# Spatial weights of the samples turned by VectorE, and a new place for the first four samples' attention values

## The chip, the core and the metric

The kernel runs on one core of a Trainium2 chip. The metric is the device time of one execution in microseconds (us), as the median over several executions; smaller is better. Before the change the three executions took 1272.37, 1272.98 and 1273.51 us, a median of 1272.98 us.

## The reference, cut to what matters

One step of a two-layer encoder for two groups of requests that share the weights: one prompt of 512 tokens, and 8 samples of 16 new tokens each. Both layers are 1024 wide with a branch of 2048.

Layer 0 mixes tokens by spatial weights. There are 16 groups of 128 channels, each with its own 128 x 128 matrix. The prompt uses the masked matrix over blocks of 128 tokens; a sample has only 16 tokens, so it uses the upper left 16 x 16 corner:

```python
wm = where(chunk_causal_mask(n)[None], w_s[:, :n, :n], 0.0)
s = einsum('gij,bnjgc->bnigc', wm, vb) + b_s[:, :n].T
y = u * s.reshape(B, T, E) * silu(z)
```

Layer 1 is attention with a forgetting bias, 16 heads of 128. The prompt attends causally to itself. Every sample attends to 256 cached rows of K and V and to its own 16 new ones:

```python
s = einsum('bqhd,bkhd->bhqk', q, k) * scale
s = s + cT[:, :, P:, None] - cT[:, :, None, :]
p = softmax(where(mask, s, -inf))
out = einsum('bhqk,bkhd->bqhd', p, v)
```

## The kernel before, in words

The tokens are five tiles of 128: four of the prompt, and one that holds the 8 samples with 16 rows each. All large matmuls take float32 operands that are split into a high and a low part, and issue three matmuls per product (`mm3`, L272, L273, L274). `split` makes the parts: ScalarE (ACT) copies the high part (L289), VectorE (DVE) subtracts it to get the low part (L290). The projections go by `seven_products`, a scheme with seven instead of eight products of quarter matrices; its sums stand on DVE (L713, L724, L726, L729) and some sums of weights on GpSimd (POOL, L211). Weights come by DMAs that POOL's queue or SyncE's (SP's) queue issues.

**Layer 0.** For each of the 16 groups g `spatial_weights(g)` makes the two right operands of `gate_spatial(g)`. The 128 x 128 matrix is loaded as it lies in memory, transposed by the TensorE (PE, L688) and copied out of PSUM (`wm`, L690, L691). For the samples, eight DMAs put the 16 x 16 corners of all groups into the tile `w16`, once for each sample's 16 partitions. `spatial_weights` multiplies one group of `w16`, repeated along the row, by a block mask on DVE (L684), which gives a block-diagonal 128 x 128 matrix `ax`. The PE transposes it (L689) and ACT copies it into `ws` (L692), the operand of the sample tile's matmul.

**Layer 1.** The heads go in eight pairs p. For p from 0 to 6 a loop interleaves the projections of this pair's gates and the next pair's V, K and Q, which are long rows of `mm3`, with short *pieces*, each of which has a due time in us from the pair's start. Pieces of the prompt: scores, softmax, turn (the PE transposes the weights, L1186) and values (L1193), block by block for each head; for the weights DVE takes a reciprocal (L1179) and scales (L1180), 128 to 512 columns wide with the block. Pieces of the samples, made by `sample_pieces(p, bg)` for two groups of four samples, bg = 0 and 1: *scores* (eight matmuls that each use 32 columns of the array, L1243, and a softmax on DVE and ACT), *turn* (three transposes, L1262), *values* (twelve matmuls of 32 columns, L1270, which are ordered one behind another) and *gate* (two transposes, L1278, and DVE L1284). The samples' K is loaded by `load_k`, transposed by DVE in 32 x 32 blocks (`turn_k`, L1219) and completed with new rows by POOL (`new_k`); V comes by `load_v`, two DMAs for four samples. `turn_v` is the PE's transposing of the next pair's projected V (L1071, L1076). The last pair's pieces are placed between the matmuls of the kernel's tail.

**Order.** A scheduler with a model of its own decides in which order the instructions of each engine go out; the due times steer it. `queued(e)` puts an instruction behind the last one issued on engine e; `tc.issue_after` says that a later instruction may not go ahead of an earlier one. Neither says that nothing else may come between. The PSUM banks of the pieces come from a ring of three (`ATT`).

## Time and profile before

| | before |
|---|---|
| median of three executions | 1272.98 us (1272.37 to 1273.51) |
| the profiled execution | 1273.51 us |
| its span from first to last instruction | 1271.6 us |
| granted PE clock | 1.00 |
| PE busy | 1264.2 us (99%) |
| DVE busy | 957.1 us (75%) |
| ACT busy | 594.6 us (47%) |
| POOL busy | 356.2 us (28%) |

The page gives for each engine the busy time, its share of the span and the number of instructions; the PE line is the sum of time in which matmuls run, and rows in a timeline are start and duration in us, engine, line, operation, the tile written and the tile read, and behind them the idle time of the engine just before with what ended it. Matmuls overlap, so the spacing of their starts tells more than their durations. Layer 0's groups with spatial weights run from about 120 to 345 us of the span, the seven pairs of heads of the loop from about 585 to 1060 us.

### The profile page before, as it was taken

To read this page: it belongs to the slowest core of one execution; us is meant where nothing else is said; L and a number is where in the kernel's file an instruction comes from. 1 tells how busy PE (TensorE), PEld (TensorE's weight loads), DVE (VectorE), ACT (ScalarE), POOL (GpSimd) and SP (SyncE) were. 2 spreads that over 40 slices of the span, in tenths; PEclk is the share of its full clock that TensorE was granted. 3 is DMA by queue.
4 is the path that set the end of the run, shared out by engine and by line. 5 is a ranking of instruction groups with operands and counts; after the bars stand their busy time and mean duration, and the time that the engine had idled before them with its cause. 6 is when DMAs were issued, how large, how long until landed. Compare 5 with 4: busy or idle time off the path is not lost.

```text
span 1271.6 us, 21433 instructions
## 1 busy us (share of the span) xinstructions
PE 1264.2 (99%) x8038; PEld 1136.5 (89%) x8038; DVE 957.1 (75%) x1795; ACT 594.6 (47%) x1076; POOL 356.2 (28%) x323
## 2 busy tenths in 40 slices
PE   9999999999999999999999999999999999999998
PEld 7888999999988888889999999999999998788887
DVE  6844999999953364789988998989898988545643
ACT  4433555544545343665445454545454445454331
POOL 1012445454000010145434535454435430000100
PEclk9999999999999999999999999999999999999999
DMA  5532343323324212657798858677888659632211
GB/s 201 174 98 78 108 127 112 103 80 104 114 94 144 94 44 84 150 127 157 173 167 168 195 150 186 157 172 142 151 168 179 177 110 283 230 129 84 67 66 50
DMA packets 275545, 171.54 MB, mean 135 GB/s; under 512 B 188721, under 2 KB 238689, under 8 KB 275442
## 3 DMA queue, kind: packets, MB, share of 16 engines
q1 hardware_dynamic: 261170, 127.80, 36.9%
q0 software_dynamic: 9760, 36.05, 13.7%
q10 hardware_dynamic: 4512, 6.33, 1.7%
q8 instruction: 63, 1.03, 0.3%
q14 instruction: 40, 0.33, 0.1%
HBM read 148.55 MB, written 21.59 MB: 134 GB/s over the span
## 4 chain that ended last, share of the span: by engine, by line
PE 97%; DVE 2%; issue 0%; ACT 0%; ACTq 0%; DVEq 0%
PE pb L272 27%; PE pb L274 27%; PE pb L273 27%; PE pb L1193 3%; PE pb L1270 2%; PE pb L419 2%; PE pb L1186 1%; PE pb L1243 1%; PE pb L317 1%; PE pb L745 1%; PE pb L1058 1%; DVE W L290 1%; PE pb L1071 1%; PE pb L1262 0%; PE pb L1059 0%
## 5 line engine op out<-in xcount | busy, mean ns | idle before, releaser
L272 PE MATMUL pb<-A,W 128*128 128x320 f32 (+1 forms) x752 | 240.7, 320 | 0.0
L273 PE MATMUL pb<-A,W 128*128 128x320 f32 (+1 forms) x752 | 233.7, 311 | 0.0
L274 PE MATMUL pb<-A,W 128*128 128x320 f32 (+1 forms) x752 | 233.2, 310 | 0.0
L290 DVE TENSOR_TENSOR W<-RAW,W 128x1024 fp32r<-128x1024 f32 (+1 forms) x122 | 149.6, 1227 | 71.9 <-ACT W L289 69.7
L273 PE MATMUL pb<-W,A 128*128 128x512 f32 x498 | 194.5, 391 | 0.0
L272 PE MATMUL pb<-W,A 128*128 128x512 f32 x498 | 194.5, 393 | 0.0
L274 PE MATMUL pb<-W,A 128*128 128x512 f32 x498 | 194.3, 391 | 0.0
L289 ACT ACTIVATE W<-RAW 128x1024 fp32r<-128x1024 f32 (+1 forms) x122 | 115.8, 949 | 90.0 <-PE pb L274 43.9
L272 PEld LDWEIGHTS pb<-A,W 128*128 128x128 f32 x752 | 141.6, 188 | 1.0 <-issue 0.2
L273 PEld LDWEIGHTS pb<-A,W 128*128 128x128 f32 x752 | 141.6, 188 | 0.5
L274 PEld LDWEIGHTS pb<-A,W 128*128 128x128 f32 x752 | 141.2, 188 | 0.0
L272 PE MATMUL pb<-tbf,W 128*128 128x320 f32 x360 | 118.9, 330 | 0.4 <-DVE R L1099 0.4
L303 POOL TENSOR_TENSOR SML<-SML 128x1 f32<-128x1 f32 x20 | 14.9, 749 | 350.9 <-DVE SML L301 346.2
L274 PE MATMUL pb<-tbf,W 128*128 128x320 f32 x360 | 111.3, 309 | 0.0
L273 PE MATMUL pb<-tbf,W 128*128 128x320 f32 x360 | 111.2, 309 | 0.0
L274 PEld LDWEIGHTS pb<-W,A 128*128 128x128 f32 x498 | 93.4, 188 | 19.6 <-issue 0.4
L273 PEld LDWEIGHTS pb<-W,A 128*128 128x128 f32 x498 | 93.6, 188 | 18.7
L272 PEld LDWEIGHTS pb<-W,A 128*128 128x128 f32 x498 | 93.5, 188 | 18.5
L211 POOL TENSOR_TENSOR sff<-RAW 128x512 f32<-128x512 f32 x46 | 61.2, 1330 | 169.3 <-DVE W L290 90.7
L713 DVE TENSOR_TENSOR R<-R,pb 128x320 f32<-128x320 f32 x184 | 86.3, 477 | 12.8 <-PE pb L274 11.7
L290 DVE TENSOR_TENSOR A<-R,A 128x640 fp32r<-128x640 f32 (+1 forms) x42 | 35.5, 880 | 57.8 <-ACT A L289 57.8
L272 PEld LDWEIGHTS pb<-tbf,W 128*128 128x128 f32 x360 | 67.7, 188 | 10.3 <-issue 5.8
(270 smaller groups left out, 2842.2 us busy)
## 6 DMA issues: line engine op xcount, KB each, us to landing
RAW<-in_fox_w_in POOLq DMA_DIRECT2D x46, 512.0 KB, 7.5
RAW<-in_gmlp_w_in SPq DMA_DIRECT2D x40, 512.0 KB
R<-in_cache_fox_k SPq DMA_DIRECT2D x128, 128.0 KB
R<-in_cache_fox_v SPq DMA_DIRECT2D x32, 512.0 KB
RAW<-in_gmlp_w_out SPq DMA_DIRECT2D x16, 512.0 KB
RAW<-in_ple_w_gate SPq DMA_DIRECT2D x16, 512.0 KB
RAW<-in_fox_w_out SPq DMA_DIRECT2D x16, 512.0 KB
R<-in_fox_w_in POOLq DMA_DIRECT2D x14, 512.0 KB, 8.5
```

What stands on the lines that cost most here:

```text
L211: nc.gpsimd.tensor_tensor(out=o, in0=a, in1=b, op=op)
L272: nc.tensor.matmul(out, lh, rh, start=start, stop=False)
L273: nc.tensor.matmul(out, lh, rl, start=False, stop=False)
L274: nc.tensor.matmul(out, ll, rh, start=False, stop=stop)
L289: first = nc.scalar.activation(out=hi, in_=src, func=AF.Copy)
L290: nc.vector.tensor_tensor(out=lo, in0=src, in1=f(hi), op=ALU.subtract)
L303: behind["pool"] = nc.gpsimd.tensor_tensor(out=q, in0=t, in1=mhalf, op=ALU.pow)
L317: behind["pe"] = nc.tensor.transpose(out=b[:, j * P:(j + 1) * P], in_=src[:, (4 * c + j) * P:(4 * c + j + 1) * P], identity=ident)
L419: line[e] = make(*args, **kw)
L713: behind["dve"] = nc.vector.tensor_tensor(out=into(i, j), in0=a, in1=b, op=ALU.add)
L1193: nc.tensor.matmul(O[:, d], v[:, j, hh * P:(hh + 1) * P], pt[:, j * P:(j + 1) * P], start=(j == 0), stop=(j == i))
L1270: last = nc.tensor.matmul(O[32 * bl:32 * bl + 32, :256], pt[:, t * P + 32 * bl:t * P + 32 * bl + 32], v_of(p)[:, 4] if t == 2 else vv[:, b ...
```

## The change

Two things are changed.

**In layer 0**, the corners are loaded so that a 32 x 32 block holds each one twice side by side (16 DMAs in place of 8), DVE transposes the whole 128 x 512 tile by 32 x 32 blocks in one instruction, and ACT copies every block's left half into `w16`. `w16` then holds turned corners, and the product with the block mask goes straight into `ws`. The 16 transposes L689 and the 16 copies L692 are gone.

**In layer 1**, for p from 0 to 6, the values of group 0 are moved from their due time 17.5 to 26.0 us, and the score matmuls of group 1 are made part of the same ordered chain: `values(products)` issues the twelve value matmuls and then, in the same `issue_after` stack, the eight score matmuls. The gate of group 0 moves from 22.5 to 28.5, the softmax of group 1 to 28.6, the load of group 1's V from 18.5 to 26.1 (it overwrites the tile that the values of group 0 read), and the two `turn_v` from 26.0 and 27.0 to 28.7 and 29.7. The softmax's reciprocal gets its own two columns in the tile `SML`. The score matmuls of every call are now in an ordered chain.

```diff
-    SML = sbuf.tile([P, N_SMALL], F32, name="SML")
+    SML = sbuf.tile([P, N_SMALL + 2], F32, name="SML")
...
+    twice, turned_twice = r1(o_u, 512), r1(o_u + 512, 512)
     for b in range(NB):
-        dma(w16[b * TS:(b + 1) * TS], w_s[0, :, :TS, :TS].rearrange("g i j -> i g j"))
+        for z in range(2):
+            dma(twice.rearrange("p (g z j) -> z p g j", g=16, z=2)[z, b * TS:(b + 1) * TS], w_s[0, :, :TS, :TS].rearrange("g i j -> i g j"))
+    with queued("dve"):
+        nc.vector.transpose(out=turned_twice, in_=twice)
+    nc.scalar.activation(out=w16, in_=turned_twice.rearrange("p (g z i) -> p g z i", g=16, z=2)[:, :, 0], func=AF.Copy)
...
         nc.vector.tensor_tensor(
-            out=ax.rearrange("p (b j) -> p b j", b=NB), in0=blk.rearrange("p (b j) -> p b j", b=NB),
+            out=ws.rearrange("p (b j) -> p b j", b=NB), in0=blk.rearrange("p (b j) -> p b j", b=NB),
             in1=w16[:, g:g + 1, :].broadcast_to([P, NB, TS]), op=ALU.mult)
         b = bank(SPA)
         nc.tensor.transpose(out=b[:, :P], in_=raw, identity=ident)
-        nc.tensor.transpose(out=b[:, P:2 * P], in_=ax, identity=ident)
...
-        nc.scalar.activation(out=ws, in_=b[:, P:2 * P], func=AF.Copy)
...
-        def scores():
-            S = bank(ATT)
+        def products(stack):
+            S = kept["S"] = bank(ATT)
+            for hh in range(2):
+                for bl in range(4):
+                    last = nc.tensor.matmul(S[32 * bl:32 * bl + 32, :272], qpads[:, hh, 4 * bg + bl].rearrange("p h q -> p (h q)"),
+                                            kt[:, hh, bl], start=(hh == 0), stop=(hh == 1))
+                    stack.enter_context(tc.issue_after(last.ins))
+
+        def weigh():
+            S = kept["S"]
...
-            m, sm, ri = small(), small(), small()
+            m, sm, ri = small(), small(), SML[:, N_SMALL + bg:N_SMALL + bg + 1]
...
-        def values():
+        def scores():
+            with ExitStack() as stack:
+                products(stack)
+            weigh()
+
+        def values(follow=None):
...
+                if follow is not None:
+                    follow(stack)
...
-    def sample_times(p, bg, t0):
-        scores, turn, values, gate = sample_pieces(p, bg)
-        return [(t0, scores), (t0 + 7.5, turn), (t0 + 12.5, values), (t0 + 17.5, gate)]
+    def sample_times(p, s0, s1):
+        scores, turn, values, gate, _, _ = sample_pieces(p, 0)
+        scores1, turn1, values1, gate1, products, weigh = sample_pieces(p, 1)
...
+        return [(s0, scores), (s0 + 7.5, turn), (s1, lambda: values(products)), (s1 + 2.5, gate), (s1 + 2.6, weigh),
+                (s1 + 7.5, turn1), (s1 + 12.5, values1), (s1 + 17.5, gate1)]
...
-                   (s0 + kb + 0.1, lambda: new_k(p, 1)), (s0 + 13.5, lambda: load_v(p, 1))]
+                   (s0 + kb + 0.1, lambda: new_k(p, 1)), ((s0 + 13.5 if p == 7 else s1 + 0.1), lambda: load_v(p, 1))]
...
-        pieces += [(26.0, lambda p=p: turn_v(p + 1, 0)), (27.0, lambda p=p: turn_v(p + 1, 1))]
+        pieces += [(28.7, lambda p=p: turn_v(p + 1, 0)), (29.7, lambda p=p: turn_v(p + 1, 1))]
```

The scheduler's rows show where the pieces come to stand. (Line numbers of the changed kernel are a few higher: L1270 becomes L1282, L1243 becomes L1244, L1186 becomes L1189, L1193 becomes L1196, L1180 becomes L1183.)

On the PE, in every pair of the loop, the values of group 0 (L1270) stood like this between projection matmuls, with two of the prompt's transposes among them:

```order
L274 MATMUL pb1_71<-A_65,W_63 128x320
L1270 MATMUL pb4_74<-R1_69 32x256 x4
L1186 MATMUL pb6_76<-CST_67,R1_69 128x128 x2
L1270 MATMUL pb4_74<-R1_69 32x256 x8
L272 MATMUL pb2_72<-tbf_4177,W_63 128x320
```

Now the values of group 0 (L1282) and, behind them, the scores of group 1 (L1244), the prompt's transposes L1189 and values L1196 stand like this:

```order
L274 MATMUL pb2_72<-A_65,W_63 128x320
L1282 MATMUL pb5_75<-R1_69 32x256 x12
L272 MATMUL pb2_72<-A_65,W_63 128x320
L1189 MATMUL pb4_74<-CST_67,R1_69 128x128 x4
L273 MATMUL pb2_72<-A_65,W_63 128x320
L274 MATMUL pb2_72<-A_65,W_63 128x320
L1196 MATMUL pb7_77<-R1_69 128x128
L1244 MATMUL pb6_76<-R1_69 32x272 x8
L1196 MATMUL pb7_77<-R1_69 128x128 x2
L272 MATMUL pb3_73<-tbf_4155,W_63 128x320
```

The twelve value matmuls are together, and five other rows stand between them and the eight score matmuls, which are inside the prompt's values.

On DVE, the stretch before the prompt's fourth block of weights (L1180, 128x512) in pair 1 was:

```order
L1179 RECIPROCAL SML_68<-SML_68 128x1
L713 TENSOR_TENSOR R1_69<-R1_69,pb3_73 128x320
L1219 STREAM_TRANSPOSE R1_69<-R1_69 128x256 x4
L1180 TENSOR_SCALAR R1_69<-R1_69,SML_68 128x512
L290 TENSOR_TENSOR W_63<-sff_4178,W_63 128x1024
L713 TENSOR_TENSOR R1_69<-R1_69,pb0_70 128x320
L1159 TENSOR_TENSOR R1_69<-CST_67 128x128
```

and is now:

```order
L716 TENSOR_TENSOR R1_69<-R1_69,pb3_73 128x320
L1222 STREAM_TRANSPOSE R1_69<-R1_69 128x256 x4
L290 TENSOR_TENSOR W_63<-sff_4156,W_63 128x1024
L1182 RECIPROCAL SML_68<-SML_68 128x1
L716 TENSOR_TENSOR R1_69<-R1_69,pb0_70 128x320
L1162 TENSOR_TENSOR R1_69<-CST_67 128x128
L1183 TENSOR_SCALAR R1_69<-R1_69,SML_68 128x512
```

The scaling of the fourth block went behind a subtraction of weights, a sum and a small operation.

On SP's queue, the loads of a pair were four of K, two of V, four of K, two of V, four of K; now they are:

```order
L124 DMA R1_69<-in_cache_fox_k 32x32x32 x4
L124 DMA R1_69<-in_cache_fox_v 128x4x256 x2
L124 DMA R1_69<-in_cache_fox_k 32x32x32 x8
L124 DMA R1_69<-in_cache_fox_v 128x4x256 x2
L124 DMA out_4<-R1_69 128x256 x4
```

The second V went behind the third load of K.

More of the change, by code (lines that the diff above doesn't have):

```diff
@@ L1285, in gate @@
                                                op0=ALU.mult, op1=ALU.mult)
-        return scores, turn, values, gate
+        return scores, turn, values, gate, products, weigh
     def prompt_times(h, t0, step):
```

11 lines of the change are left out of this document (5 added, 6 removed).

## Prediction

> **What bounds the kernel now.** I read the page first: span, busy shares and the chain of work that ended last.
>
> ```profile
> span 1271.6 us, 21433 instructions
> PE 1264.2 (99%) x8038; PEld 1136.5 (89%) x8038; DVE 957.1 (75%) x1795; ACT 594.6 (47%) x1076; POOL 356.2 (28%) x323
> PE 97%; DVE 2%; issue 0%; ACT 0%; ACTq 0%; DVEq 0%
> ```
>
> The PE is busy for 1264.2 of 1271.6 us and carries 97% of the chain. So a row taken off the PE shortens the kernel unless another engine steps in, and a row elsewhere costs only if it makes the PE wait. The two stages that the change touches come from the view by windows (window and length, then busy us and rows of PE, weight loads, DVE, ACT, POOL, then granted clock, DMA share and GB/s):
>
> ```profile
> 120.00:345.00 225.00, 224.53 (x1561) 222.63 (x1560) 210.44 (x329) 118.93 (x217) 93.52 (x61) 1.00 0.35 107
> 585.06:1059.74 474.68, 474.49 (x3628) 444.41 (x3627) 417.82 (x966) 228.56 (x454) 211.38 (x205) 1.00 0.78 165
> ```
>
> The first holds the sixteen groups of layer 0, the second the seven pairs of heads. In both the PE is full and at full clock, but DVE is close behind: 210.44/225.00 = 94% and 417.82/474.68 = 88%. Every term below is therefore PE time, and every danger is a DVE row that comes late.
>
> **Term a: sixteen transposes fewer.** One of them in the PE's timeline, between projection matmuls, and the group of all sixteen:
>
> ```profile
> 140.20 0.31 PE L274 MATMUL pb<-tb,W 128*128 128x320 f32 x1
> 140.49 0.31 PE L273 MATMUL pb<-A,W 128*128 128x320 f32 x1
> 140.64 0.31 PE L274 MATMUL pb<-A,W 128*128 128x320 f32 x1
> 140.79 0.27 PE L689 MATMUL pb<-CST,R 128*128 128x128 f32 x1
> 141.04 0.31 PE L273 MATMUL pb<-A,W 128*128 128x320 f32 x1
> L689 PE MATMUL pb<-CST,R x16: 270/270/272, 140.8 to 336.4; 128*128 128x128 f32 x16
> ```
>
> The row says 0.27 us, but matmuls overlap and the spacing of starts is what counts. From an L274 to the second row after it takes 140.49 − 140.20 = 0.29 us without a transpose, and 141.04 − 140.64 = 0.40 with L689 between. One costs 0.11; rounding leaves 0.10 to 0.11, and 16 × 0.105 gives **−1.7 us**. Whether the PE can use this depends on DVE:
>
> ```profile
> 142.42 0.49 DVE L726 TENSOR_TENSOR R<-R,pb 128x320 f32<-128x320 f32 x1 [0.58 <-PE pb L274]
> ```
>
> DVE waits 0.58 us for the PE's L274 just after this transpose. So it is the PE that is late there, and I book the whole term; its bounds are −1.7 and 0 (a rival below).
>
> **What term a adds** is hidden. The new DVE transpose reads 128x512; the nearest row is the larger block transpose of the 128x640:
>
> ```profile
> L1085 DVE STREAM_TRANSPOSE R<-R 128x640 f32<-128x640 f32 x16 | 13.3, 831 | 0.0
> ```
>
> So it costs under 0.83 us, once, near 126 us; the 0.58 us of DVE idle time above, and others like it, stand behind it. If that cover were gone it would cost the PE 0.83 us at most. ACT gains one copy and loses sixteen. The eight further DMAs are issued by SP's queue:
>
> ```profile
> 69.45 0.33 SPq L124 DMA_DIRECT2D R<-in_gmlp_b_s  x1
> 75.53 3.98 SPq L124 DMA_DIRECT2D RAW<-in_gmlp_w_in  x2
> ```
>
> At 0.33 us each, as the first row, they take 2.6 us, and between 69.45 + 0.33 = 69.78 and 75.53 the queue does nothing. Their data are wanted some 50 us later. I take 0.
>
> **Term b: the values of group 0 in one piece.** Before, two of the prompt's transposes split the twelve value matmuls of group 0 (the same order in all seven pairs); those of group 1 stand together. Pair 0 of the loop, both groups:
>
> ```profile
> 599.96 0.31 PE L274 MATMUL pb<-A,W 128*128 128x320 f32 x1
> 600.20 0.64 PE L1270 MATMUL pb<-R 128*32 128x256 f32 x8
> 600.77 0.44 PE L1186 MATMUL pb<-CST,R 128*128 128x128 f32 x2
> 601.13 1.07 PE L1270 MATMUL pb<-R 128*32 128x256 f32 x16
> 602.39 0.31 PE L273 MATMUL pb<-tbf,W 128*128 128x320 f32 x1
> ...
> 631.86 0.31 PE L274 MATMUL pb<-A,W 128*128 128x320 f32 x1
> 633.79 0.31 PE L273 MATMUL pb<-tbf,W 128*128 128x320 f32 x1
> ```
>
> Both times I measure from the L274 ahead to the L273 behind. Split: 602.39 − 599.96 = 2.43 us. Together: 633.79 − 631.86 = 1.93. Of the difference, 0.50, the two transposes are 2 × 0.105 = 0.21, which stay in the program; 0.29 is the price of entering and leaving 32-column work once more. Seven pairs: 7 × 0.29 = **−2.0 us**. The bounds are 0, if the new place splits them in another way, and −2.0; the printed order shows the twelve in one piece, so I take all of it.
>
> The Trainium skill (TensorEngine Tiling (Array Packing), Key Properties) says that a change of the tiling mode drains the TensorE. The 0.29 us agrees; the page has no price. By its rule the change's second half would pay too if the scores really followed the values, which is the rival "tied" below.
>
> **Term c: the scores leave into other work.** The order puts the eight scores of group 1 inside the prompt's values (L1196, two passes per matmul) instead of ahead of the transposes L1071. So the exit changes its neighbour. What that costs is not shown in the same place; nearest are values of the prompt alone and two-pass matmuls right behind scores:
>
> ```profile
> 613.38 0.83 PE L1193 MATMUL pb<-R 128*128 128x128 f32 x6
> 614.13 1.12 PE L1243 MATMUL pb<-R 128*32 128x272 f32 x16
> ...
> 1093.90 0.49 PE L1163 MATMUL pb<-R 128*128 128x128 f32 x2
> 1094.23 0.83 PE L1193 MATMUL pb<-R 128*128 128x128 f32 x6
> ```
>
> A row of the first kind takes (614.13 − 613.38)/6 = 0.125 us, so two take 0.25; behind scores two take 1094.23 − 1093.90 = 0.33. The exit costs 0.08 at most more than into transposes, and nothing if those pay it too: 0 to 7 × 0.08 = 0.6. With no reason for either end I take the middle, **+0.3 us**.
>
> **Term d: the prompt's fourth weights come later on DVE.** The order moves L1180 (128x512) behind L290, L713 and L1159. Pair 1 before on DVE, the four transposes L1186 that wait for it on the PE, and the same two in pair 2:
>
> ```profile
> 677.89 0.44 DVE L1180 TENSOR_SCALAR R<-R,SML 128x512 f32<-128x512 f32 x1
> 678.25 1.21 DVE L290 TENSOR_TENSOR W<-sff,W 128x1024 fp32r<-128x1024 f32 x1
> 679.39 0.47 DVE L713 TENSOR_TENSOR R<-R,pb 128x320 f32<-128x320 f32 x1
> 679.79 0.28 DVE L1159 TENSOR_TENSOR R<-CST 128x128 f32<-128x128 f32 x1
> 679.99 0.34 DVE L1284 SCALAR_TENSOR_TENSOR R<-pb,R 128x64 f32<-128x64 f32 x2
> ...
> 680.25 0.60 PE L1186 MATMUL pb<-CST,R 128*128 128x128 f32 x4
> ...
> 745.14 0.44 DVE L1180 TENSOR_SCALAR R<-R,SML 128x512 f32<-128x512 f32 x1
> ...
> 748.00 0.60 PE L1186 MATMUL pb<-CST,R 128*128 128x128 f32 x4
> ```
>
> The three rows now ahead take 679.99 − 678.25 = 1.74 us from start to start. The weights would start at 677.89 + 1.74 = 679.63 and end, after 0.44, at 680.07. The PE reached the transposes at 680.25; with the 0.29 of term b and two transposes (0.21) gone from ahead of it and one row (0.15, the spacing of 140.49 and 140.64) added, it arrives at 679.90: 0.17 us too early. In pair 2 the weights end at 745.14 + 1.74 + 0.44 = 747.32 and the PE comes at 748.00 − 0.35 = 747.65, which is 0.33 in time. Queued behind the moved row on DVE are sums of the projections and the smaller scores' rows; behind the waiting transposes on the PE is all of the projection. One pair late by 0.17 and one in time make 0.08 on average, times 7: **+0.5 us**, between 0 and 2.4 (all seven late by 0.17 and as much again for the hand-over, 0.34).
>
> **The moved V load.** It overwrites the tile that the values of group 0 read, so it goes out after them, and on SP's queue behind the third K load:
>
> ```profile
> 677.99 9.01 SPq L124 DMA_DIRECT2D R<-in_cache_fox_k  x4
> ...
> 699.85 1.50 PE L1270 MATMUL pb<-R 128*32 128x256 f32 x24
> ...
> R<-in_fox_w_in POOLq DMA_DIRECT2D x14, 512.0 KB, 8.5
> ```
>
> The K load's last issue ends at 677.99 + 9.01 = 687.00; V's two transfers, of 512 KB each, are wanted at 699.85. That leaves 12.8 us. The last row, from the list of DMA issues, is another transfer of that size: a median of 8.5 us from issue to landing. Side by side two of them fit; one after the other they take 17 and the PE would stand for 4.2 (a rival below). With the DMA engines busy for 0.78 of this stage there is room, and I take 0. The gate, the softmax and `turn_v` only move to later times with the same rows; `turn_v` is wanted by the next pair, tens of us later, and the softmax of group 1 by its turn at 33.5, some 5 us behind its scores. I take 0 for them.
>
> **Sum.** −1.7 − 2.0 + 0.3 + 0.5 = −2.9 us. The profiled execution took 1273.51 us (span 1271.6 and 1.9 around it), so its like would be at 1270.6. It was the slowest of the three, 0.5 above the median of 1272.98; from the median I predict **1270.1 us**. What a measurement here can tell from no change is about 0.2%, 2.5 us: below 1270.43 counts as faster, above 1275.53 as slower.
>
> **Rivals.**
>
> *DVE is late in every pair.* The fourth weights come late by 0.34 in all seven pairs, 2.4 us for the 0.5 of term d: 1270.1 + 1.9 = 1272.0. For it: DVE is 88% busy there and pair 1 is short already. Against it: pair 2 has 0.33 to spare.
>
> *Layer 0 is bound by DVE.* Then the PE waits where a transpose was and term a is 0: 1271.8. For it: 94% busy. Against it: DVE idles on the PE in the row at 142.42.
>
> *The stretch is really tied.* If nothing stood between the values and the scores on the chip's path, seven more entries and exits would go, again 7 × 0.29 = 2.0 us: 1268.1. Against it: the printed order has five rows in between, and engines execute in that order.
>
> *POOL stops DVE ahead of the fourth weights: slower.* This one is a single place, the L290 that the order has put ahead of the weights. A like row of the same line took three times as long when POOL was at work:
>
> ```profile
> 672.64 1.86 DVE L290 TENSOR_TENSOR W<-R,W 128x512 fp32r<-128x512 f32 x1
> 675.49 0.68 DVE L290 TENSOR_TENSOR W<-R,W 128x512 fp32r<-128x512 f32 x1
> ...
> 672.63 1.31 POOL L211 TENSOR_TENSOR sff<-RAW 128x512 f32<-128x512 f32 x1
> ```
>
> The price is 1.86 − 0.68 = 1.2 us. If the shifted times brought a POOL row beside that L290 in every pair, the weights would be 1.2 later and the PE would wait for all of it: 7 × 1.2 = 8.4 on top, 1278.5. It turns the gain to a loss from 2.9/7 = 0.41 us per pair, and past 0.2% from 5.4/7 = 0.77. Against it: the L290 at 678.25 took its 1.21 undisturbed, 4 us after POOL's row ended. The Trainium skill (SBUF — State Buffer, SBUF: two separate sides) says why: a DVE instruction with two SBUF inputs and a GpSimd instruction that reads SBUF take a shared port in turns, and the later one waits. The pair of rows agrees.
>
> *The V load is late: slower.* If the two transfers went one after the other, the PE would stand for 4.2 us in each pair, 29 us: 1299. Against it: the free fifth of the DMA engines' time, and that the two are issued together.
>
> **How the numbers follow.** The forecast 0.60; DVE late in every pair 0.13; layer 0 bound by DVE 0.10; POOL 0.08; tied 0.05; V late 0.04. The likeliest one's own range is 1269.3 to 1271.1 (term c from 0 to 0.6, term d from 0 to 1.2); about three quarters of it lie below 1270.43. Faster: 0.75 × 0.60 + 0.05 = 0.50. Slower: 0.08 + 0.04 = 0.12. The rest, 0.15 + 0.13 + 0.10 = 0.38, is no change to be told. The range from 1268.0 to 1274.0 holds the forecast, the tied case and both cases near 1272, 0.88 in all; its upper end stands for POOL in a pair or two.
>
> **What would show it.** Term a: no second transposes in the first window, and 1.7 us less from its first to its last group; if DVE binds, a longer idle of the PE that ends with a DVE row. Term b: the spacing from the row ahead of the twelve values to the second row behind them, 1.93 in place of 2.43. Term c: two L1196 rows behind the scores, 0.33 against 0.25. Term d: the idle time ahead of the four transposes L1189 in each pair, ended by DVE L1183: 0 to 0.2 us. V: no idle time of the PE ahead of group 1's values that a DMA ends. The prediction is wrong if the period of the pairs, from one group-0 turn to the next, does not shrink by 0.2 us or so, or if a new idle of the PE of over 0.4 us stands in each pair.

## The result and the profile after

The change made the kernel slower: 1294.17 us median (1290.88 to 1295.28) against 1273.24 us for the kernel before on the same chip (1272.37 to 1274.01). The ratio is 1.016 with a 95% interval of 1.0146 to 1.0174, or 20.9 us more; 1270.1 was forecast. The profiled execution took 1290.88 us with a span of 1289.0, which is 17.4 us over the 1271.6 of before. It is the fastest of the four, with a mean granted clock of 0.997; the other three have 0.995.

The page of the kernel after, busy shares and chain:

```profile
PE 1268.0 (98%) x8022; PEld 1137.2 (88%) x8022; DVE 964.9 (75%) x1796; ACT 592.9 (46%) x1061; POOL 347.6 (27%) x323
PE 83%; DVE 11%; issue 3%; DMA 1%; ACT 1%; SPq 0%; DVEq 0%; ACTq 0%
```

The PE's share of the chain fell from 97% to 83%, and DVE's rose from 2% to 11%. The two stages of the change, in the windows of the kernel after (columns as before; the second now ends at 1077 us):

```profile
120.00:345.00 225.00, 222.94 (x1543) 220.74 (x1542) 211.91 (x327) 116.45 (x202) 91.11 (x61) 1.00 0.35 107
585.00:1077.00 492.00, 479.75 (x3655) 448.67 (x3654) 426.73 (x974) 231.16 (x458) 206.37 (x208) 0.99 0.79 161
```

In the second the PE stands for 492.00 − 479.75 = 12.3 us; before it was busy for 474.49 of 474.68. What it waits for, by the PE's waits after (us in total, times, longest):

```profile
PE pb L1189 <- DVE R L1183: 10.2, 6, 2.2
PE pb L1244 <- DVE SML L1175: 2.0, 4, 0.5
...
PE pb L272 <- DVE R L727: 1.3, 2, 0.7
PE pb L272 <- DVE R L729: 0.7, 3, 0.2
```

The first row holds the wait that term d spoke of: the four transposes of the prompt's fourth block of weights wait for the scaling L1183. Five of the six waits, 8.4 of the 10.2 us, are this one (2.24, 1.50, 1.70, 1.48 and 1.50 us), where term d had 0.5 for all pairs; the sixth, 1.81 us, is for an earlier block in pair 0. Where in the loop the loss falls is seen from pair to pair. The first transpose of group 0 in a pair serves as a mark; here in the PE's timeline of before and of after:

```profile
594.18 0.49 PE L1262 MATMUL pb<-CST,R 128*128 128x128 f32 x3
661.92 0.49 PE L1262 MATMUL pb<-CST,R 128*128 128x128 f32 x3
...
1000.66 0.49 PE L1262 MATMUL pb<-CST,R 128*128 128x128 f32 x3
```

```profile
595.48 0.49 PE L1269 MATMUL pb<-CST,R 128*128 128x128 f32 x3
668.01 0.49 PE L1269 MATMUL pb<-CST,R 128*128 128x128 f32 x3
...
1014.97 0.49 PE L1269 MATMUL pb<-CST,R 128*128 128x128 f32 x3
```

The distances between such marks, worked out for all of them:

| us | to the first mark | pair 0 | 1 | 2 | 3 | 4 | 5 | 6 | last mark to end of span |
|---|---|---|---|---|---|---|---|---|---|
| before | 594.18 | 67.74 | 67.75 | 67.75 | 67.74 | 67.75 | 67.75 | 73.29 | 197.65 |
| after | 595.48 | 72.53 | 67.50 | 69.79 | 70.98 | 71.19 | 67.50 | 74.91 | 199.12 |
| difference | +1.3 | +4.8 | −0.25 | +2.0 | +3.2 | +3.4 | −0.25 | +1.6 | +1.5 |

The differences add up to the 17.4 us. Pairs 1 and 5 gained 0.25 us each, which is what terms b and c gave (1.7/7 = 0.24). It comes from the rows that the prediction named; the values of group 0 in pair 1 after:

```profile
684.04 0.31 PE L274 MATMUL pb<-A,W 128*128 128x320 f32 x1
684.28 1.50 PE L1282 MATMUL pb<-R 128*32 128x256 f32 x24
...
685.97 0.60 PE L1189 MATMUL pb<-CST,R 128*128 128x128 f32 x4
```

From the row ahead to the second row behind them it is 685.97 − 684.04 = 1.93 us, as term b had it. All other pairs lost, and 2.8 us went outside them.

**Why pairs 2, 3, 4 and 6 are late and pairs 1 and 5 are not.** First DVE, POOL and the PE in pair 2 after, in three timelines:

```profile
750.92 1.18 DVE L290 TENSOR_TENSOR W<-sff,W 128x1024 fp32r<-128x1024 f32 x1
752.03 0.14 DVE L1182 RECIPROCAL SML<-SML 128x1 f32<-128x1 f32 x1
752.10 0.46 DVE L716 TENSOR_TENSOR R<-R,pb 128x320 f32<-128x320 f32 x1
752.48 1.12 DVE L1162 TENSOR_TENSOR R<-CST 128x128 f32<-128x128 f32 x1
753.52 1.55 DVE L1183 TENSOR_SCALAR R<-R,SML 128x512 f32<-128x512 f32 x1
```

```profile
752.18 1.28 POOL L211 TENSOR_TENSOR sff<-RAW 128x512 f32<-128x512 f32 x1 [5.13 <-DVE SML L1182]
753.53 1.26 POOL L211 TENSOR_TENSOR sff<-sff,RAW 128x512 f32<-128x512 f32 x1
754.87 1.35 POOL L211 TENSOR_TENSOR sff<-RAW,sff 128x512 f32<-128x512 f32 x1
```

```profile
755.13 0.66 PE L1189 MATMUL pb<-CST,R 128*128 128x128 f32 x4 [1.50 <-DVE R L1183]
...
756.81 1.12 PE L1244 MATMUL pb<-R 128*32 128x272 f32 x16 [0.51 <-DVE SML L1175]
```

The L290 at 750.92 reads `sff`, the tile into which POOL writes its sums of weights. It ends at 750.92 + 1.18 = 752.10, and at 752.18 POOL starts three sums in a row (the trace names the small row L1182 behind L290 as the releaser). They meet DVE's L1162 (1.12 us) and the weights L1183 (1.55 us). In pair 5 POOL's sums came after the weights; DVE and POOL after:

```profile
963.10 0.28 DVE L1162 TENSOR_TENSOR R<-CST 128x128 f32<-128x128 f32 x1
963.30 0.47 DVE L1183 TENSOR_SCALAR R<-R,SML 128x512 f32<-128x512 f32 x1
```

```profile
967.87 1.29 POOL L211 TENSOR_TENSOR sff<-RAW 128x512 f32<-128x512 f32 x1 [10.21 <-DMA RAW<-in_fox_w_in]
```

POOL needs `sff` free and its weights loaded, whichever is later; here it was the load. Undisturbed, the two DVE rows take 0.28 and 0.47 us, so the meeting costs 0.84 + 1.08 = 1.9 us in pair 2. In pair 1, too, the weights were undisturbed (0.48) and POOL's sums came behind them, at 687.90.

The Trainium skill (SBUF — State Buffer, SBUF: two separate sides) says that the port DVE and GpSimd share is an exclusive lock that the first to start holds for its whole instruction. The trace agrees: L1162, which started at 752.48 while POOL's first sum was running, ended at 753.60, just behind that sum's end at 753.46. The weights and POOL's second sum start 0.01 us apart, so their starts do not tell which came first; the weights are longer by 1.08 us, somewhat less than one POOL row.

**The clock.** In pair 3 the wait was 1.70 us, and the loss is larger than the wait. Two windows of the kernel after, behind the waits of pairs 3 and 4, and the score rows of pair 3:

```profile
825.60:828.90 3.30, 3.30 (x23) 1.75 (x21) 2.87 (x8) 2.19 (x6) 2.06 (x3) 0.50 1.10 327
897.30:900.60 3.30, 3.05 (x21) 1.76 (x22) 2.29 (x6) 2.19 (x6) 1.12 (x2) 0.50 1.14 325
```

```profile
826.79 2.04 PE L1244 MATMUL pb<-R 128*32 128x272 f32 x16
```

The granted clock is 0.50 there for 3.3 us, and the sixteen score rows take 2.04 us, where the same rows took 1.12 in pair 2 above. In pair 4 they took 2.04 as well. So pairs 3 and 4 lose 3.2 and 3.4 us, and pair 2, with its clock kept, 2.0. What lets the clock fall is not the length of the wait alone: it fell behind 1.70 and 1.48 us in pairs 3 and 4, and not behind 2.24, 1.50 and 1.50 in pairs 0, 2 and 6. In the trace of `e2_layer1` (below) it fell behind 2.22, 1.50 and 1.48 us, and not behind 1.49 and 1.50.

### The profile page after: what moved, and what is told of

Same layout as the page of the kernel before. It is cut to its first block, busy times and chain, and to the rows that moved or that the text cites. A ratio compares the mean times of both kernels' runs of the same rounds, so it can differ in the third digit from the quotient of the medians.

```text
span 1289.0 us, 21387 instructions
## 1 busy us (share of the span) xinstructions
PE 1268.0 (98%) x8022; PEld 1137.2 (88%) x8022; DVE 964.9 (75%) x1796; ACT 592.9 (46%) x1061; POOL 347.6 (27%) x323
## 4 chain that ended last, share of the span: by engine, by line
PE 83%; DVE 11%; issue 3%; DMA 1%; ACT 1%; SPq 0%; DVEq 0%; ACTq 0%
PE pb L272 23%; PE pb L274 23%; PE pb L273 23%; DVE W L290 3%; PE pb L1196 3%; PE pb L419 2%; PE pb L1244 1%; PE pb L1282 1%; DVE R L716 1%; DVE R L1222 1%; DVE R L1126 1%; PE pb L317 1%; PE pb L1189 1%; PE pb L748 1%; PE pb L1061 1%
## 5 line engine op out<-in xcount | busy, mean ns | idle before, releaser
L272 PE MATMUL pb<-A,W 128*128 128x320 f32 (+1 forms) x752 | 240.7, 320 | 1.3 <-DVE R L727 1.3
L274 PE MATMUL pb<-A,W 128*128 128x320 f32 (+1 forms) x752 | 233.6, 311 | 0.0
L273 PE MATMUL pb<-A,W 128*128 128x320 f32 (+1 forms) x752 | 233.1, 310 | 0.0
L290 DVE TENSOR_TENSOR W<-RAW,W 128x1024 fp32r<-128x1024 f32 (+1 forms) x122 | 147.4, 1209 | 73.7 <-ACT W L289 66.5
L273 PE MATMUL pb<-W,A 128*128 128x512 f32 x498 | 194.6, 391 | 0.0
L272 PE MATMUL pb<-W,A 128*128 128x512 f32 x498 | 194.6, 393 | 0.0
L274 PE MATMUL pb<-W,A 128*128 128x512 f32 x498 | 194.5, 392 | 0.0
L272 PEld LDWEIGHTS pb<-A,W 128*128 128x128 f32 x752 | 141.6, 188 | 5.3 <-issue 3.1
L273 PEld LDWEIGHTS pb<-A,W 128*128 128x128 f32 x752 | 141.7, 188 | 0.2
L274 PEld LDWEIGHTS pb<-A,W 128*128 128x128 f32 x752 | 141.3, 188 | 0.1
L272 PE MATMUL pb<-tbf,W 128*128 128x320 f32 x360 | 116.1, 323 | 0.4 <-DVE R L1102 0.4
L273 PE MATMUL pb<-tbf,W 128*128 128x320 f32 x360 | 111.9, 311 | 0.0
L274 PE MATMUL pb<-tbf,W 128*128 128x320 f32 x360 | 111.7, 310 | 0.0
L274 PEld LDWEIGHTS pb<-W,A 128*128 128x128 f32 x498 | 93.4, 188 | 19.6 <-issue 0.4
L273 PEld LDWEIGHTS pb<-W,A 128*128 128x128 f32 x498 | 93.6, 188 | 18.9
L272 PEld LDWEIGHTS pb<-W,A 128*128 128x128 f32 x498 | 93.5, 188 | 18.5
L1178 ACT ACTIVATE R<-R,SML 128x128 f32<-128x128 f32 (+1 forms) x64 | 35.9, 561 | 135.9 <-DVE SML L1175 135.9
L290 DVE TENSOR_TENSOR A<-R,A 128x640 fp32r<-128x640 f32 (+1 forms) x42 | 35.5, 880 | 57.7 <-ACT A L289 57.7
```

The source lines that it names most:

```text
L272: nc.tensor.matmul(out, lh, rh, start=start, stop=False)
L273: nc.tensor.matmul(out, lh, rl, start=False, stop=False)
L274: nc.tensor.matmul(out, ll, rh, start=False, stop=stop)
L290: nc.vector.tensor_tensor(out=lo, in0=src, in1=f(hi), op=ALU.subtract)
L1178: nc.scalar.activation(out=pr[:, :n], in_=pr[:, :n], func=AF.Exp, scale=-1.0, bias=m, accum_out=sm)
```

## The experiments

All times are medians; the ratio is against the kernel before, run beside it, with its 95% interval. It need not equal the quotient of two medians. "Pairs" are the distances between marks as above.

### The two parts apart

**The part in layer 0 alone** (`e1_layer0`): the diff's lines of layer 0 without the rest, `SML` as before.

> Only the change in layer 0 (weights' corners turned by VectorE, sixteen PE transposes and ACT copies gone); layer 1 as before. Theory DVE-bound (from the trace after: the PE now waits 0.67 us for DVE in two places of that stage, and the stage's length went from 212.7 to 213.0 us): the time stays within 0.5 us of before, 1273 us. Rival, term a of the prediction: 1.7 us less, about 1271.5 us.

Measured: 1279.87 against 1273.62 beside it, ratio 1.0043 [1.0029, 1.0058], +6.2 us. Pair 0 took 76.03 (+8.3), the others 67.75 but for one of 68.89. The part neither gained in layer 0 nor was neutral behind it.

**The part in layer 1 alone** (`e2_layer1`): all the other lines, `SML` two columns longer included.

> Only the change in layer 1 (values of group 0 moved and tied ahead of the scores of group 1); layer 0 as before. Theory: all of the loss is here, 1290 to 1295 us, with idle time of the PE ahead of the transposes L1189 in five pairs or more, 1.5 to 2.2 us each. Rival: the loss has a part in layer 0 or in how both act together, then clearly less than 1290 us.

Measured: 1292.93, ratio 1.0146 [1.0114, 1.0177]. Pairs 75.91, 67.50, 69.77, 71.33, 71.35, 67.50, 74.90, the pattern of the whole change. The loss in the pairs behind pair 0 comes from this part.

### The late weights

**The next weights' split is held behind the prompt's fourth weights** (`e3_weights_first`), otherwise as `e2_layer1`:

```diff
-            nc.vector.tensor_scalar(out=pr[:, :n], in0=pr[:, :n], scalar1=ri, ...)
+            w = nc.vector.tensor_scalar(out=pr[:, :n], in0=pr[:, :n], scalar1=ri, ...)
+            if i == 3 and hh == 0:
+                behind["w4"] = w
...
-                split(...)
+                with ExitStack() as stack:
+                    if "w4" in behind:
+                        stack.enter_context(tc.issue_after(behind.pop("w4").ins))
+                    split(...)
```

> The change in layer 1 alone, with one order put back: the first subtraction of weights (L290) that is issued after the prompt's fourth block of softmax weights must stand behind that block's scaling on DVE. The scheduler then puts the scores of group 1 right behind the values of group 0 and splits these six and six. Theory late weights (DVE's scaling behind L290, and POOL's sums that L290 releases stop it): the idle time ahead of the four transposes is gone, 1272 to 1274 us. Rival, that moving or tying values and scores costs by itself (V load, bank, softmax later): 1285 us or more.

Measured: 1278.37, ratio 1.0038 [1.0022, 1.0055]; 14.6 us below `e2_layer1`. DVE and POOL in pair 2 of it (L293 here is the L290 of before):

```profile
750.85 0.28 DVE L1162 TENSOR_TENSOR R<-CST 128x128 f32<-128x128 f32 x1
751.05 0.48 DVE L1183 TENSOR_SCALAR R<-R,SML 128x512 f32<-128x512 f32 x1
751.45 1.22 DVE L293 TENSOR_TENSOR W<-sff,W 128x1024 fp32r<-128x1024 f32 x1
```

```profile
752.79 1.28 POOL L211 TENSOR_TENSOR sff<-RAW 128x512 f32<-128x512 f32 x1 [6.25 <-DVE W L293]
```

With the row that reads `sff` behind the weights, POOL's sums start behind them too. The waits for the fourth weights are gone in all seven pairs; in pair 0 (73.05) two waits of 1.2 and 2.0 us for earlier DVE rows are left. With them and with the shifted layout (below) the expected 1272 to 1274 us were missed. This order splits the values of group 0 into six and six with the transposes between, and pairs 1 to 5 take 67.85 and not 67.50. By the spacing of starts, in pair 2 of this run against pair 1 after, the values and transposes take 0.29 us more, the price of term b. The scores, two of which stand ahead of the last two values, take 0.35 more, and the other rows 0.29 less; so the period is not the count of entries alone.

**POOL's sums shortened to 64 of 512 columns** (`e4_short_pool`), otherwise as `e2_layer1`, the order of DVE unchanged:

```diff
+                    if i > S2 + 4:
+                        o, a, b = o[:, :, :16], a[:, :, :16], b[:, :, :16]
                     nc.gpsimd.tensor_tensor(out=o, in0=a, in1=b, op=op)
```

> The change in layer 1 alone, in the order of the change, with POOL's sums of weights in layer 1 cut to 64 of 512 columns from the second set on; the rest of each sum is left out, so what the projections of heads compute is not the reference's. Theory POOL's lock: DVE's scaling of 128x512 takes 0.45 to 0.5 us in every pair in place of 1.55, the PE no longer waits there, 1270 to 1273 us. Rival, DVE's own three rows ahead of the scaling (1.74 us) are enough: about 0.8 us of idle time per pair stays, 1276 us or more.

Measured: 1280.5, ratio 1.0051 [1.0033, 1.007], not the expected 1270 to 1273; the shifted layout (below) is in it. Pairs 69.70, four of 67.50, 70.35, 72.63; the weights took 0.54 to 0.61 us in every pair. The three rows that the order put ahead of the weights are still there, and four pairs are as short as pairs 1 and 5 of the change: it is POOL's meeting DVE that decides, not the rows ahead. Pair 5 is late for another reason: the PE waited 2.64 us for the weights, because a block transpose of DVE further ahead had waited for its K:

```profile
952.73 1.43 DVE L1221 STREAM_TRANSPOSE R<-R 128x256 f32<-128x256 f32 x4 [4.72 <-DMA R<-in_cache_fox_k]
```

### Layer 0

**Before, with sixteen DVE rows less in layer 0** (`e6_before_light_dve`), and **the layer-0 part on top of that** (`e7_layer0_light_dve`):

```diff
-        nc.vector.scalar_tensor_tensor(out=spb[z], in0=spb[z], scalar=lnb[:, g:g + 1], in1=r1(o_bs + z * P, P), op0=ALU.mult, op1=ALU.add)
```

> The kernel before without the sixteen DVE rows L683 (the scaling of the added spatial bias is left out). Read in the stage of layer 0 alone, from the first L688 to the last L746: 212.7 us before. Theory DVE-bound: with some 6 us of DVE gone, the three waits of 0.3 us go, about 211.7 us. It is the base for the next run.

> The change in layer 0 alone, also without the sixteen scalings on DVE. Same stage, against the run before this one. Theory DVE-bound: with DVE lighter the sixteen transposes are worth what the prediction said, 1.7 us less than the base. Rival, that a transpose in the stream is worth less than 0.105 us: no difference again.

Measured: 1273.47, ratio 1.0006 [0.9992, 1.002], and 1278.75, ratio 1.0041 [1.0021, 1.0061]. From the first transpose of layer 0's groups to their last matmul, worked out from the traces: before 212.64, after 212.97, `e6` 212.51, `e7` 211.87. Without the change the lighter DVE gives the PE nothing to speak of (−0.1). With it, taking the transposes away is worth 0.64 of the 1.7 us. Both are less than was expected. In the view of waits for layer 0 (120 to 345 us) before had this one row:

```profile
PE pb L272 <- DVE R L726: 0.3, 2, 0.2
```

After, the same window has the two rows L272 <- L727 and L729 quoted in the first section, 1.3 + 0.7 = 2.0. The PE's busy time fell from 224.53 to 222.94 us, so the transposes were worth about what term a said, and the waits for DVE grew by 1.7 us, as much. With the lighter DVE the waits are 0.2 us in `e6` and 0.7 in `e7`. So DVE takes the gain of term a; that a lighter DVE gives back only 0.64, with waits of only 0.5 more, leaves some 0.5 us of the 1.7 without an account. One of the waits, PE and DVE after, and the same DVE row before:

```profile
187.11 0.38 PE L693 MATMUL pb<-CST,R 128*128 128x128 f32 x2
188.16 0.41 PE L272 MATMUL pb<-A,W 128*128 128x320 f32 x1 [0.67 <-DVE R L727]
```

```profile
187.63 0.47 DVE L727 TENSOR_TENSOR R<-R,pb 128x320 f32<-128x320 f32 x1
```

```profile
187.62 0.47 DVE L724 TENSOR_TENSOR R<-R,pb 128x320 f32<-128x320 f32 x1
```

DVE's sum ends at the same instant in both kernels. The PE reaches this place 1.0 us earlier and stands; 0.6 of that come from the stage's earlier start (130.7 in place of 131.3), 0.2 from the two transposes gone by then.

### What the two columns and the eight loads cost

**Nothing but a comment** (`e9_copy`) measures what two equal kernels differ by.

> The kernel before with one line of comment more, so that only line numbers behind it change; a control. Theory that the neutral run's loss came from its extra instruction or its memory layout: 1273 to 1274 us. Rival, that the loss in the first pair has nothing to do with what the program does (the way it lies in memory, or when it is built): 1277 to 1281 us, the same as the neutral run.

Measured: 1273.81, ratio 0.9996 [0.9984, 1.0009].

**Before, with `SML` two columns longer and a write of zeros into them by POOL** (`e5_neutral`), and **with the two columns alone** (`e10_wider`):

```diff
-    SML = sbuf.tile([P, N_SMALL], F32, name="SML")
+    SML = sbuf.tile([P, N_SMALL + 2], F32, name="SML")
...
+    nc.gpsimd.memset(SML[:, N_SMALL:N_SMALL + 2], 0.0)
```

(The last line is in `e5_neutral` only.)

> The kernel before with one small memset more on POOL at the start of layer 0 (two columns that nothing reads); all engines' other rows in the same order. In the runs of layer 0 alone and of the weights-first order the first pair of heads took 5 to 8 us longer, its PE waiting for DVE rows that came late after a DMA, and no row was moved ahead of that place. Theory tight start: the kernel before is only just in time there, and any change of its program or timing can lose that; then 1276 to 1280 us, or some of its runs there. Rival, that the loss in the first pair comes from what the change does: 1273 us, like before.

> The kernel before with the tile SML two columns wider and nothing else: the tiles behind it lie 8 bytes further. It parts the two things that the neutral run added. If the layout on chip is what loses the first pair: 1277 to 1281 us; if it is the extra POOL instruction: 1273 to 1274 us.

Measured: 1281.05, ratio 1.005 [1.0035, 1.0065], and 1281.45, ratio 1.0045 [1.0028, 1.0062]. They agree, so the write of zeros adds nothing. In `e10_wider` no instruction differs from the kernel before, and in the traces the PE, DVE, POOL and SP's queue have the same rows in the same order. All that differs is that the tile R1, and everything that lies behind `SML`, starts 8 bytes further on in each partition. In the median that costs 7.8 us (1281.45 against 1273.68 beside it). The twelve executions fall into two groups, four of 1275.69 to 1277.70 and eight of 1280.87 to 1283.73. The trace is of the first group and has pair 0 on time (67.72); that of `e5_neutral`, an execution of 1284.08, has 73.26 there. Two effects can be read. First the DMA queue of the page (packets, MB, share of 16 engines), of before, of `e10_wider`:

```profile
q1 hardware_dynamic: 261170, 127.80, 36.9%
```

```profile
q1 hardware_dynamic: 261170, 127.80, 38.5%
```

The same packets take more time. By the packet records, the 172,032 packets of 128 bytes among them take 14.6 ns on average in place of 13.0 (14.8 in the kernel after, 12.9 in `e1_layer0`, which has the old layout). Second, 512-column matmuls, with the tile as right operand in the two stages ahead of and behind the pairs (min/median/max ns, first and last start); before:

```profile
L272 PE MATMUL pb<-W,r2x_t x80: 387/389/398, 464.1 to 528.2; 128*128 128x512 f32 x80
L272 PE MATMUL pb<-W,r2z_t x88: 277/389/397, 1204.1 to 1266.6; 128*128 128x512 f32 x72, 128*128 128x256 f32 x16
```

and after the whole change:

```profile
L272 PE MATMUL pb<-W,r2x_t x80: 392/395/403, 463.8 to 529.4; 128*128 128x512 f32 x80
L272 PE MATMUL pb<-W,r2z_t x88: 277/395/400, 1220.1 to 1284.0; 128*128 128x512 f32 x72, 128*128 128x256 f32 x16
```

From first to last start it is 65.6 us in place of 64.1, and 63.9 in place of 62.5. Those 1.5 and 1.4 us are the 1.3 ahead of the first mark (the stage began 0.3 earlier, at 463.8) and the 1.5 behind the last one. `e10_wider` has 65.6 and 63.8. From start to start the three rows of one product (L272, L273, L274) take 0.70 us in place of 0.68.

**The whole change with `SML` 16 columns longer, so that R1 moves by 64 bytes** (`e13_after_aligned`); the two below it are variants of the next section with the same line.

```diff
-    SML = sbuf.tile([P, N_SMALL + 2], F32, name="SML")
+    SML = sbuf.tile([P, N_SMALL + 16], F32, name="SML")
```

> The whole change with one number other: SML is 16 columns wider than before in place of 2, so that the tiles behind it move by 64 bytes in place of 8. The run with SML two columns wider alone lost 7.7 us, with 14.6 in place of 13.0 ns for each 128-byte packet and the same bytes. Theory layout: the 128-byte packets are back at 13.0 ns and the time falls by 4 to 8 us to 1286 to 1290 us; what stays is the late softmax weights. Rival, that late weights are all of it: 1293 us as the change.

> The truly tied order with weights first, and SML 16 columns wider in place of 2. If layout is what made the first pair late in the run with 2: a median of 1269 to 1271 us (67.16 us in the pairs, 4 us under the kernel before). Rival: the first pair is late in this order anyway, 1277 to 1279 us.

> The same with the second half of the first V load later. Theory: 1269 to 1270 us, with fewer slow runs than without the move. Rival, that the move does nothing once the layout is right: equal to the run without it.

Measured: 1292.39, ratio 1.0133 [1.0111, 1.0154]; 1276.38, 1.0008 [0.9993, 1.0023]; 1275.71, 1.0008 [0.9993, 1.0023]. The packets of 128 bytes still took 14.5 ns, and the three 512-column rows of a product 0.70 us. In both a shift by 64 bytes is as slow as one by 8, and the theory that 8 bytes are the odd amount fell. The medians lie about 2 us below those with 8 bytes (1294.17 for the change, 1278.38 for `e8_truly_tied` below); why is not shown. `e13_after_aligned` also shows the weight of the clock: its one execution with a mean granted clock of 1.00 took 1285.22 us, the five with 0.995 took 1289.70 to 1293.89.

The Trainium skill (DMA: Bandwidth & Descriptors, How a descriptor splits into AXI transactions) says that a descriptor's transactions start at multiples of 256 bytes, and that one which does not start there pays for bytes it does not use. Before, R1 starts at byte 100,736 by the sizes of the tiles ahead of it, a multiple of 128. Packets of 128 bytes at multiples of 128 never cross a multiple of 256; shifted by 8 or by 64 bytes, every second one does. That would fit both measured shifts, but the page speaks of reads, and the shift by 128 bytes that would settle it was not tried.

**Before, with eight further loads of the corners that nothing uses** (`e16_eight_more_loads`):

```diff
+        dma(twice.rearrange("p (g z j) -> z p g j", g=16, z=2)[0, b * TS:(b + 1) * TS], w_s[0, :, :TS, :TS].rearrange("g i j -> i g j"))
```

> The kernel before with the eight further loads of corners alone, into a place that nothing reads. The change in layer 0 alone lost 6 us in the first pair of heads without any move of tiles. If the further loads on SP's queue do it: 1277 to 1281 us. Rival, that it is the changed timing of layer 0 or the DVE transpose: 1273 to 1274 us, as before.

Measured: 1278.07 against 1273.97 beside it, ratio 1.0026 [1.0015, 1.0037], +4.1 us. The rows of PE, DVE and POOL and their order are those of before, and SP has eight rows more; the 128-byte packets stay at 13.0 ns. Pair 0 took 72.37. So eight loads, issued at 64 to 69 us, cost 4 us at 600 us, and are a good part of what `e1_layer0` lost in pair 0.

What is late ahead of pair 0 can be read from DVE's rows that wait for a transfer, in `e16_eight_more_loads`, in `e3_weights_first` and in the kernel after:

```profile
585.85 0.49 DVE L728 TENSOR_TENSOR R<-R,pb 128x320 f32<-128x320 f32 x1 [1.99 <-DMA out<-R]
```

```profile
583.07 1.19 DVE L1253 TENSOR_TENSOR R<-R,CST 128x16 f32<-128x16 f32 x1 [1.91 <-DMA R<-cs_sc]
```

```profile
583.15 0.18 DVE L1251 TENSOR_TENSOR R<-R,CST 128x16 f32<-128x16 f32 x1 [0.65 <-DMA R<-cs_sc]
588.49 0.49 DVE L729 TENSOR_TENSOR R<-R,pb 128x320 f32<-128x320 f32 x1 [1.49 <-DMA out<-R]
```

Before has no such row between 575 and 592 us. There the DMA engines are nearly full (a share of 0.93 from 576 to 584 us before, 0.99 after), while POOL issues weights, SP the samples' K and ACT's queue the small load of `cs_sc`. In the kernel after `cs_sc` was issued behind POOL's weights, at 575.28 against 574.62 us; before it was ahead of them, at 572.95 against 573.32. The order of issue cannot be the whole reason: in `e7_layer0_light_dve` it was 0.06 us ahead of them, and DVE still waited 2.93 us for it. DVE falls some 2 us back, and the PE's waits for it in pair 0 follow (1.81 us at 604.09 in the kernel after, where the scaling that it waits for also took 1.35 us beside a sum of POOL, against 0.35 in `e4_short_pool`). Why eight early loads change what is late half a millisecond later is not shown.

### Which version beats both

**The values and the scores really tied, with the weights first** (`e8_truly_tied`): `e3_weights_first` with the due time of the joined stretch a microsecond earlier, at which the order has nothing left between the two.

```diff
-        pieces = attention_pieces(p, 4.8, 26.0) + next_keys(p + 1, 34.0, 46.2)
-        pieces += [(28.7, ... turn_v(p + 1, 0)), (29.7, ... turn_v(p + 1, 1))]
+        pieces = attention_pieces(p, 4.8, 25.0) + next_keys(p + 1, 34.0, 46.2)
+        pieces += [(27.7, ... turn_v(p + 1, 0)), (28.7, ... turn_v(p + 1, 1))]
```

> The change in layer 1 alone, with the weights ahead of the subtraction as in the weights-first run, and values, scores and what hangs on them due 1 us earlier (25.0): the order then has the twelve values and the eight scores side by side with nothing between in all seven pairs. By the prediction's price of 0.29 us for one entry and exit, twice: a period of 67.75 - 0.58 = 67.2 us in the pairs after the first. Rival, that the price is only paid at one side: 67.5. In total 1269 us, or 1273 if the first pair loses 4 to 5 us again.

Measured: 1278.38, ratio 1.0039 [1.0022, 1.0055]; pairs 70.90, five of 67.16, 72.29. The undisturbed pairs gain 0.59 us, as expected. The rest of the kernel loses more, with the layout still shifted.

**A later load of V at the start of layer 1**, in the kernel before (`e11_before_later_v`) and in `e8_truly_tied` (`e12_tied_later_v`): the second DMA of the first pair's V goes out behind the next four loads of K.

```diff
-        ... (6.0, lambda: load_v(0, 0))])
+        ... (12.2, lambda: new_k(0, 0)), (8.2, lambda: load_v(0, 0))])
```

> The kernel before with the second half of the first cached V load moved behind the first K load of the next group on SP's queue, out of the stretch from 576 to 584 us where the DMA engines are busy all the time; it is wanted at 600. Theory crowded start (the mask of the first samples, K and the weights race there): the stretch loses 0.5 MB and the first pair is on time, 1273 us in most runs. Rival: the later V load itself makes values of group 0 wait, 1276 us or more.

> The truly tied order with the same move of the V load (its values are wanted only at 611 us here). Theory crowded start: the first pair's waits (1.6 and 2.3 us in the run without the move) shrink, the other pairs keep 67.16 us: 1269 to 1273 us. Rival, that the first pair's loss has another cause: as before the move, a median near 1278 us.

Measured: 1273.33, ratio 0.9999 [0.9984, 1.0013], and 1274.27, ratio 1.0008 [0.9992, 1.0024]. It does nothing where the layout is the old one, and the second time lies 4.1 us below `e8_truly_tied`. With the shift by 64 bytes, where the packets are as slow, the same move was worth only 0.7 (1276.38 to 1275.71 above). So that slower packets hurt at the start of layer 1 is likely, but not shown.

**The old layout** (`e17_tied_same_layout`): `e8_truly_tied` with the reciprocal in two free columns of R1 and `SML` as before; and the same with the later V (`e18_tied_same_layout_later_v`).

```diff
-    SML = sbuf.tile([P, N_SMALL + 2], F32, name="SML")
+    SML = sbuf.tile([P, N_SMALL], F32, name="SML")
...
-            m, sm, ri = small(), small(), SML[:, N_SMALL + bg:N_SMALL + bg + 1]
+            m, sm, ri = small(), small(), r1(o_w1 + P + bg, 1)
```

> The truly tied order with weights first and the tile SML as wide as before: the two columns for the reciprocals lie in a free place of R1. With SML 2 or 16 columns wider (8 or 64 bytes) the 128-byte packets took 14.5 ns; R1 began at a multiple of 128 bytes in the kernel before. Theory that it is the 128-byte boundary: 13.0 ns a packet again, the first pair on time in most runs, a median of 1269 to 1271 us. Rival, that the order itself makes the first pair late: 1276 us, as with 16 columns.

> The same with the second half of the first V load later. Theory: 1269 to 1270 us in nearly all runs, the fastest so far. Rival, that the move does nothing with the old layout: equal to the run beside it.

Measured: 1270.14 (1268.21 to 1278.17) against 1274.02, ratio 0.9982 [0.9965, 0.9999], and 1271.3, ratio 0.9991 [0.9976, 1.0007]. The first is faster than both kernels of this document, than the one before by little: its interval ends just under one, and that of the second, the same order with the later V, does not. Three of its twelve executions took 1276 us or more. The 128-byte packets are back at 13.0 ns, and in the profiled execution pairs 0 to 5 take 67.17. Two of its marks, and the tied stretch of pair 2:

```profile
659.82 0.49 PE L1271 MATMUL pb<-CST,R 128*128 128x128 f32 x3
726.99 0.49 PE L1271 MATMUL pb<-CST,R 128*128 128x128 f32 x3
```

```profile
742.39 1.50 PE L1284 MATMUL pb<-R 128*32 128x256 f32 x24
743.71 1.10 PE L1246 MATMUL pb<-R 128*32 128x272 f32 x16
```

The values (24 rows) run straight into the scores, with no other row between. From `e8_truly_tied` to this one 8.2 us are gone, which agrees with the 7.8 of `e10_wider`; by the ratios it is 7.3 and 5.7.

**The sum.** In the trace of the kernel after, 14.6 of the 17.4 us lie in the pairs. The PE's waits there are 10.2 + 2.0 = 12.2 us; the two stretches at a clock of 0.50 cost some 1.7 each by estimate, half of their 3.3; the pairs' gain of 7 × 0.25 takes 1.8 off. That makes 13.8 of the 14.6. By the medians of the runs, the late weights cost about 14.6 us (`e2` to `e3`) and the shifted layout about 7.8 (`e10`), less 1.8: 20.6 of the 20.9 measured; the layer-0 part on top of `e2` adds 1.2, within the spread. This second agreement is better than the parts deserve: the 7.8 is a median over two groups of executions, executions of `e2` alone lie between 1284.64 and 1300.23, `e3` pays 0.10 per pair where `e2` gains 0.25, and the layout and the eight loads both fall on pair 0 and do not add there.

## Why the prediction was wrong, point by point

**What bounds the kernel: right.** The PE was full, and every loss inside the loop begins with a DVE row that came late, as the first part said. That the clock would fall behind such a wait was not in it.

**Term a (−1.7): wrong.** The price of a transpose was about right (1.6 us less of busy PE), but the stage did not get shorter: the rival "layer 0 is bound by DVE", at 0.10, came true. The step that failed is reading one wait, the 0.58 us at 142.42, as the state of the whole stage. DVE was busy for 94% there, and the PE's waits on DVE rose by those same 1.7 us. A lighter DVE freed 0.64 of it.

**What term a adds, taken as 0: wrong for the eight loads.** The block transpose was hidden: the first transpose of the groups stands at 130.7, against 131.3 before. The loads were, too, in layer 0, of which the prediction spoke, but eight of them in the kernel before cost 4.1 us at the start of layer 1.

**Terms b and c (−2.0 + 0.3): right per pair.** The undisturbed pairs took 67.50, 0.25 us less, for a forecast of 0.24, and the stretch of the values took the 1.93 us that term b had. The middle that term c took, without a reason for either end, was near by luck: behind the scores four rows L1196 take 0.47 us from start to start, four L1071 there took 0.41 before.

**Term d (+0.5, between 0 and 2.4): this is the step that cost most.** It summed the durations of the rows now ahead, from pair 1, and had the weights 0.17 us late there. In pair 1 after they were not late at all. It missed what one of those rows releases: L290 is the last reader of `sff`, so with it POOL's three sums move ahead of the weights as well. The measured price is 8.4 us of waits for the weights in five pairs, 1.5 in pair 2, and 2.0 more at the scores behind them, with the clock halved in two of the pairs.

**The POOL rival (8.4 us, at 0.08): the right mechanism in the wrong row.** It was argued for the L290 itself and ruled out by the L290 of pair 1, "4 us after POOL's row ended". The row that is hit is not L290 but what follows it, and in pair 1 POOL waited for a load instead (its sum at 685.63 before). That the waits for the weights add up to the rival's 8.4 us is chance: it had 1.2 in each of seven pairs, and they were 1.48 to 2.24 in five. The trace of before had it in pair 2, DVE and POOL:

```profile
745.50 1.22 DVE L290 TENSOR_TENSOR W<-sff,W 128x1024 fp32r<-128x1024 f32 x1
747.03 1.21 DVE L1159 TENSOR_TENSOR R<-CST 128x128 f32<-128x128 f32 x1
```

```profile
746.79 1.30 POOL L211 TENSOR_TENSOR sff<-RAW 128x512 f32<-128x512 f32 x1 [5.59 <-DVE W L290]
```

The releaser of POOL's sum is that L290, and the row behind it, L1159, took 1.21 us in place of 0.28. Before, the weights (745.14) were already through. The same is in pairs 3, 4 and 6 of before; these and pair 0 are the pairs whose weights were stopped, though in pair 0 before POOL still waited for a load. A second pair of the same timeline shows it.

**What was not priced at all: the two columns of `SML`.** The diff shows them in its first line. They were taken as a place for two numbers, and move everything that lies behind: 7.8 us in the median of `e10_wider`.

**The V load (0) and its rival: right.** No row of the PE waits for V. **The rival "tied"** did not happen in the change, as argued, but its price was right: 0.29 more per pair was worked out, and in `e8_truly_tied` the pairs gained 0.59 in all; in `e3_weights_first`, where values and scores mix, they gained nothing. **DVE late in every pair** was also not the case: with POOL's sums short (`e4_short_pool`) and the same rows ahead of the weights, four pairs took 67.50.

## What to carry to other kernels

When an order moves an instruction ahead of another, list not only how long it takes but what it releases: a buffer that comes free earlier starts another engine earlier, and that engine may stop the very instruction that was moved back. Read the rows of one period in several periods before using one as evidence, since here the pair that was looked at was the exception. And a tile that grows by a few bytes moves all that is allocated behind it; new small values are better put into free columns, or the growth is measured by itself.

## What was not expected of the hardware

- With R1 starting 8 or 64 bytes further on, 128-byte DMA packets took 14.5 to 14.9 ns in place of 13.0, and three 512-column float32 matmuls that read a shifted tile 0.70 us in place of 0.68. Which multiple is needed, and why the matmuls slow down, stays open.
- A 128x512 scaling on DVE that took 0.47 us alone took 1.55 with POOL's sums beside it, and a 128x128 product 1.12 in place of 0.28.
- A wait of the PE of 1.70 us was followed by 3.3 us at a granted clock of 0.50, which nearly doubled the time of sixteen score rows (2.04 against 1.12 us). One of 1.48 us did the same, one of 2.24 us did not, and what decides is open.
- Eight unused loads at 64 to 69 us made a stage at 600 us 4 us longer, with the rows of PE, DVE and POOL in the same order.
